# Half of the context's weight remainders formed on VectorE instead of GpSimd, in a two-layer RWKV-7 and neighbourhood-attention block

## The chip, the cores and the metric

One core of one Trainium2 chip runs the whole program in one launch. The metric is the device time of that launch in microseconds, as the median of the runs shown. Engines are named as in the profile: PE is TensorE's matrix multiply, PEld its weight load, DVE is VectorE, ACT is ScalarE, POOL is GpSimd, SP is SyncE, which issues most of the DMAs.

## The reference, cut to what matters

Two layers work on 512 latent tokens (`x`) and, in the first layer only, on 256 context tokens (`ctx`), both 1024 wide. Layer 0 projects both streams with the same weights, scans them in both directions (RWKV-7, 12 heads), projects back and runs a SwiGLU feed-forward net; layer 1 is neighbourhood attention of the latents, with the context's keys and values in the same softmax, and a feed-forward net again.

```python
def swiglu(h, w1, w3, w2):
    return (jax.nn.silu(h @ w1) * (h @ w3)) @ w2
...
    p_lat = h @ w_in
    p_ctx = hc @ w_in
...
        if want_ctx:
            xc = layer_norm(ALPHA * xc + gc_m * yc, ln_g[i, 0], ln_b[i, 0])
            hc = xc * (1.0 + scc_f) + shc_f
            xc = layer_norm(ALPHA * xc + gc_f * swiglu(hc, ffn_w1[i], ffn_w3[i], ffn_w2[i]), ln_g[i, 1], ln_b[i, 1])
```

## The kernel before

**Products in three parts.** Every large product is made with operands split in two: a rounded part `hi` (type fp32r) and the remainder `lo = raw - hi`. `mm3` (L118) multiplies `hi*hi` (L123), `hi` of the weights with `lo` of the activations (L124) and `lo` of the weights with `hi` of the activations (L125). So each weight slice, 128 x 512 in most cases (four blocks of 128 rows by 128 columns), takes four steps: a DMA from SP's queue into `wraw`, a copy on ACT into `whi`, a subtraction into `wlo`, and twelve matmuls.

**Two places do this.** In layer 0's projections, `project` (L246) asks `weight` (L113) for the two slices of one column of `w_in`, and `split` (L104) copies on ACT (L109) and subtracts on GpSimd (L110): 23 columns for the context and the same 23 for the latents, 92 slices. `wraw` has three buffers there, `whi` and `wlo` two each. Everywhere else a `Flow` (L844), one for the context and one for the latents, asks its own `weight` (L878) and `fetch` (L883) for slices; it copies on ACT (L887) and subtracts on `self.lo` (L888), which is GpSimd for the context (`stream` is 1) and VectorE for the latents:

```python
        self.lo = kern.nc.gpsimd if stream else kern.nc.vector
...
        self.lo.tensor_tensor(out=lo, in0=raw, in1=hi, op=ALU.subtract)
```

The context's `Flow` has 176 slices with GpSimd: 16 for the output projection (`mixer_out`, L988), 88 for the feed-forward net's `w1` and `w3`, 72 for its `w2` (`ffn`, L1015), whose 22 blocks are taken by 5, 5, 5, 5 and 2. A column of five blocks is a slice of four and one of a single block (128 x 128), one of two blocks is a slice of 128 x 256. `wraw`, `whi` and `wlo` have three buffers each. When the context's keys and values for layer 1 are made, L610 sets its `self.lo` to VectorE.

**What sets the order.** Each piece of work is given a level by `self.level` (L84); the framework (`schedule_with_timeline_sim=True`) simulates the engines and writes a fixed order of instructions for each of them, a lower level first. An engine then runs its own list strictly in order. The stages of layer 0 are written out in `STAGES` (L26) and woven by `emit` (L513): projections of the context, with the RWKV jobs of the context between them, then projections of the latents, with the context's scan. The latents' scan (`chain`, L1273, level 0, and `prep`, L1071, level 2) then runs in six jobs, and the context's `Flow` (level 8, L595) lies beside it as work of low level. Evacuations of its PSUM bank, with two halves under the one tag `s`, are at level 1 (`gated` L904, `sl` L1028 and L1029). The latents' `Flow` follows at level 9.

Of the kernel before, what the change touches and what calls it, by code (L numbers as in the profile page):

```python
# [12 lines left out]
ALU = mybir.AluOpType  # L13
# [3 lines left out]
P = 128  # L17
# [1 line left out]
NX_, NT_, NS_, NAR_, NA1_, NR_, NY_ = 2, 5, 4, 1, 4, 3, 4  # L19
ND_, NK_, NBK_, NGO_, NAW_ = 6, 3, 2, 3, 4  # L20
ADA0 = 12
POOL_LO = 1

SETS = 9 * "0123"

# [48 lines left out]
class Kernel:  # L74
    def __init__(self, ctx, tc, a, out):
        self.ctx, self.tc, self.nc, self.a, self.out = ctx, tc, tc.nc, a, out
        self.now = 0
        self.tail = None
        self.ps = {}
        self.const = ctx.enter_context(tc.tile_pool(name="const", bufs=1))  # L80
        self.wp = ctx.enter_context(tc.tile_pool(name="wp", bufs=2))
# [19 lines left out]
            "p (%s) -> p %s" % (" ".join(names), " ".join(names)), **dict(zip(names, shape))  # L101
        )

    def split(self, raw, shape, tag="w", bufs=2, pool=None):  # L104

        pool = pool or self.split_pool
        hi = pool.tile(shape, F32R, name=tag + "hi", tag=tag + "hi", bufs=bufs)
        lo = pool.tile(shape, F32R, name=tag + "lo", tag=tag + "lo", bufs=bufs)
        self.nc.scalar.copy(out=hi, in_=raw)  # L109
        (self.nc.gpsimd if POOL_LO else self.nc.vector).tensor_tensor(out=lo, in0=raw, in1=hi, op=ALU.subtract)  # L110
        return hi, lo

    def weight(self, src, shape):  # L113
        raw = self.wp.tile(shape, F32, name="wraw", tag="wraw", bufs=3)
        self.nc.sync.dma_start(out=raw, in_=src)
        return self.split(raw, shape, bufs=2)

    def mm3(self, ps, l, r, first, last, after=None):  # L118
        (lh, ll), (rh, rl) = l, r
# [126 lines left out]
    def project(self, h, src, piece, done):  # L246

        off, n, st = piece
        with self.level(self.now - 1):
            w = [self.weight(src[:, 4 * i:4 * i + 4, :], [P, 4, P]) for i in range(2)]  # L250
        t = self.bank("g", (n,))
        for k in range(KD):
            wk = tuple(x[:, k % 4, :] for x in w[k // 4])
            self.mm3(t, wk, h[1 - st](k), k == 0, k == KD - 1)
            yield n / T
        with self.level(self.now - 1):
            done(t)
# [206 lines left out]
    def gemm(self, h, p, piece):  # L464
# [6 lines left out]
        def project(ft, name):  # L471
            t = self.go(name, n)
            yield from self.project(h, a.w_in[ft], piece, self.shift_mix(ft, t))
            nc.sync.dma_start(out=self.rkv_d[ft][st], in_=t)
            return t
        k = yield from project(6 + p, "k")
        with self.level(self.now - 1):
            sq = self.go("sq", n)
            nc.scalar.activation(out=sq, in_=k, func=AF.Square, scale=col)
        yield from project(12 + p, "v")  # L480
        with self.level(self.now - 1):
            pn = self.bank("g", (nt, 2))
            for t in range(nt):
# [6 lines left out]
                scalar2=0.0, op0=ALU.mult, op1=ALU.add,  # L490
            )
        yield from project(p, "r")
        with self.level(self.now - 1):
            pe = self.bank("g", (n,))
# [345 lines left out]
class Flow:  # L840
# [3 lines left out]
    def __init__(self, kern, pool, prefix, off, n, stream, banks, bg, slots, wide=None):  # L844
        self.K, self.nc, self.pool, self.prefix = kern, kern.nc, pool, prefix
        self.ahead, self.ev = (CAHEAD, CEV) if stream else (LAHEAD, LEV_)
        self.off, self.n, self.stream, self.banks, self.bg = off, n, stream, banks, bg
        self.slots, self.turn, self.halves = slots, 0, []
        self.lo = kern.nc.gpsimd if stream else kern.nc.vector
        wide = self.wide = wide or pool  # L850
        self.xz = wide.tile([P, KD, n], F32, name=prefix + "xz")
        self.h = tuple(wide.tile([P, KD, n], F32R, name=prefix + s) for s in ("hhi", "hlo"))
# [24 lines left out]

    def weight(self, src, shape):  # L878
        tile = lambda s, t: self.wide.tile(shape, t, name="w" + s, tag=self.prefix + "w" + s, bufs=self.slots["w" + s])
        with self.K.level(self.ahead):  # L880
            return self.fetch(tile, src, shape)

    def fetch(self, tile, src, shape):  # L883
        raw = tile("raw", F32) if self.stream else self.K.wp.tile(shape, F32, name="wraw", tag="wraw", bufs=3)
        hi, lo = tile("hi", F32R), tile("lo", F32R)
        self.nc.sync.dma_start(out=raw, in_=src)
        self.nc.scalar.copy(out=hi, in_=raw)  # L887
        self.lo.tensor_tensor(out=lo, in0=raw, in1=hi, op=ALU.subtract)  # L888
        return hi, lo

    def column(self, ps, src, nk, act, order=None, after=None):
# [607 lines left out]
```

## Time and profile before

| | |
|---|---|
| runs shown | 2381.03, 2384.98, 2388.77 us; median 2384.98 |
| the profiled execution | 2381.51 us; span 2379.5 us |
| busy share of the span | PE 91%, PEld 73%, DVE 52%, ACT 42%, POOL 28% |
| granted clock of TensorE, mean | 0.937 |
| instructions | 44426 |

The profile's span runs from the first to the last instruction, so 2.0 us of the profiled execution lie outside it. Busy shares are over the whole span; the stages differ, and the windows below give them apart. A row of waits has the engine, line and tile that waited, what ended the wait, the total in us, how often, and the longest.

### The profile page before, as it was taken

Reading aid. Unit: us, or ns where it says so; the run is one execution under the profiler, and the core shown is the slowest. Engines: PE = TensorE matmul, PEld = TensorE weight load, DVE = VectorE, ACT = ScalarE, POOL = GpSimd, SP = SyncE. Lnnn points to the kernel's source line nnn. Section 1 sums busy time; section 2 is a strip of 40 time slices with the busy share of each in tenths; the row PEclk is TensorE's granted clock in tenths of the full one; section 3 lists DMA queues with packets and bytes.
Section 4 is the critical chain, followed back from the end, with each engine's and each line's share of the span. In section 5 each row is a group of like instructions: output and inputs, shape, how many; then the busy total and the mean of one; then the engine's idle time right before and its main releaser. Section 6 shows DMA issues by size and latency. Waiting matters only on the chain.

```text
span 2379.5 us, 44426 instructions
## 1 busy us (share of the span) xinstructions
PE 2163.1 (91%) x16944; PEld 1735.9 (73%) x16944; DVE 1226.7 (52%) x2529; ACT 994.5 (42%) x2075; POOL 660.5 (28%) x643
## 2 busy tenths in 40 slices
PE   6787988889879898979999999998999998999995
PEld 4676666556657777757788887787878876888874
DVE  2666555636746764244534453347556665333343
ACT  3545344444534544334443342224455644322332
POOL 2442213121322433456642310005224442000021
PEclk9889999879879899999999999999999998999997
DMA  7766476666753544576544335332432112333331
GB/s 262 224 187 188 121 205 186 175 176 187 228 142 89 137 128 112 169 233 214 162 150 118 116 120 167 113 91 88 133 105 63 51 63 66 97 92 100 96 90 63
DMA packets 324677, 327.34 MB, mean 138 GB/s; under 512 B 137328, under 2 KB 214768, under 8 KB 324464
## 3 DMA queue, kind: packets, MB, share of 16 engines
q1 hardware_dynamic: 320720, 317.45, 45.1%
q10 hardware_dynamic: 2592, 3.90, 0.5%
q8 instruction: 133, 2.18, 0.4%
q0 software_dynamic: 1152, 3.15, 0.3%
q14 instruction: 80, 0.66, 0.1%
HBM read 280.02 MB, written 42.80 MB: 136 GB/s over the span
## 4 chain that ended last, share of the span: by engine, by line
PE 62%; DVE 6%; DMA 5%; issue 2%; ACT 2%; SPq 1%; POOL 1%; POOLq 0%; ACTq 0%; DVEq 0%
PE y L123 7%; PE y L125 7%; PE y L124 7%; PE w L123 6%; PE w L124 6%; PE w L125 6%; PE s L123 3%; PE s L125 3%; PE s L124 3%; PE s L743 1%; PE w L1157 1%; DMA wraw<-w 1%; PE v L201 1%; PE v L725 1%; PE y L700 1%
## 5 line engine op out<-in xcount | busy, mean ns | idle before, releaser
L887 ACT CAST whi<-wraw 128x512 fp32r<-128x512 f32 (+2 forms) x560 | 330.2, 594 | 674.1 <-PE y L124 261.0
L888 DVE TENSOR_TENSOR wlo<-wraw,whi 128x512 fp32r<-128x512 f32 (+2 forms) x384 | 293.1, 767 | 339.6 <-ACT whi L887 316.1
L888 POOL TENSOR_TENSOR wlo<-wraw,whi 128x512 fp32r<-128x512 f32 (+2 forms) x176 | 202.3, 1155 | 299.4 <-ACT whi L887 270.7
L123 PE MATMUL w<-lhhi,whi 128*128 128x512 f32 x472 | 189.3, 403 | 11.3 <-ACT lhhi L1012 5.8
L110 POOL TENSOR_TENSOR wlo<-wraw,whi 128x512 fp32r<-128x512 f32 x92 | 121.4, 1323 | 280.1 <-ACT whi L109 233.3
L123 PE MATMUL y<-lhhi,whi 128*128 128x512 f32 x488 | 192.3, 394 | 0.5 <-ACT lhhi L752 0.5
L124 PE MATMUL y<-lhlo,whi 128*128 128x512 f32 x488 | 190.7, 391 | 0.0
L125 PE MATMUL y<-lhhi,wlo 128*128 128x512 f32 x488 | 190.6, 391 | 0.0
L124 PE MATMUL w<-lhlo,whi 128*128 128x512 f32 x472 | 186.4, 395 | 1.3 <-DVE lhlo L937 1.1
L125 PE MATMUL w<-lhhi,wlo 128*128 128x512 f32 x472 | 185.6, 393 | 0.1
L913 POOL TENSOR_TENSOR lxz<-lxz,s 128x512 f32<-128x512 f32 x28 | 43.3, 1578 | 508.9 <-ACT s L919 508.9
L123 PE MATMUL s<-chhi,whi 128*128 128x256 f32 x480 | 145.5, 303 | 19.6 <-DVE kclo L616 7.8
L123 PE MATMUL g<-hhi,whi 128*128 128x256 f32 (+1 forms) x368 | 139.1, 378 | 17.4 <-DVE nr L486 4.5
L125 PE MATMUL s<-chhi,wlo 128*128 128x256 f32 x480 | 143.2, 298 | 1.1 <-POOL wlo L888 1.1
L124 PE MATMUL s<-chlo,whi 128*128 128x256 f32 x480 | 143.3, 299 | 0.4 <-DVE chlo L937 0.4
L125 PE MATMUL g<-hhi,wlo 128*128 128x256 f32 (+1 forms) x368 | 135.6, 369 | 2.2 <-POOL wlo L110 2.1
L124 PE MATMUL g<-hlo,whi 128*128 128x256 f32 (+1 forms) x368 | 132.6, 360 | 0.0
L123 PEld LDWEIGHTS s<-chhi,whi 128*128 128x128 f32 x480 | 97.2, 203 | 29.9 <-ACT whi L887 8.8
L123 PEld LDWEIGHTS w<-lhhi,whi 128*128 128x128 f32 x472 | 89.2, 190 | 36.0 <-ACT lhhi L984 7.4
L123 PEld LDWEIGHTS y<-lhhi,whi 128*128 128x128 f32 x488 | 92.1, 189 | 22.1 <-issue 3.0
L124 PEld LDWEIGHTS w<-lhlo,whi 128*128 128x128 f32 x472 | 89.3, 189 | 23.6 <-DVE lhlo L937 4.2
L125 PEld LDWEIGHTS y<-lhhi,wlo 128*128 128x128 f32 x488 | 91.9, 188 | 19.8 <-DVE n L937 0.8
(376 smaller groups left out, 5048.3 us busy)
## 6 DMA issues: line engine op xcount, KB each, us to landing
wraw<-w SPq DMA_DIRECT2D x368, 256.0 KB, 2.6
aw<-ada_w SPq DMA_DIRECT2D x128, 256.0 KB, 4.7
wraw<-w_in SPq DMA_DIRECT2D x92, 256.0 KB, 3.3
bk<-bk SPq DMA_DIRECT2D x72, 256.0 KB, 4.3
wraw<-ada_w SPq DMA_DIRECT2D x64, 256.0 KB, 3.4
wraw<-w_out SPq DMA_DIRECT2D x48, 256.0 KB, 3.0
wraw<-wk SPq DMA_DIRECT2D x32, 256.0 KB, 2.9
wraw<-wv SPq DMA_DIRECT2D x32, 256.0 KB, 3.1
```

The source lines that it names most:

```text
L110: (self.nc.gpsimd if POOL_LO else self.nc.vector).tensor_tensor(out=lo, in0=raw, in1=hi, op=ALU.subtract)
L123: mm(ps, lhsT=lh, rhs=rh, start=first, stop=False)
L124: mm(ps, lhsT=lh, rhs=rl, start=False, stop=False)
L125: self.last = mm(ps, lhsT=ll, rhs=rh, start=False, stop=last)
L201: mm = nc.tensor.matmul(ps[32 * q:32 * q + 32, part], lhsT=self.cs[:, k + q, :], rhs=w[q // step][:, q % step, :], start=k == 0, stop=k > ...
L700: return lambda: mm(banks[j][:, 256 * c:256 * c + 256], lhsT=q[i == 2][hd, cb * P:cb * P + P], rhs=r[i == 1][hd, cs], start=i == 0, stop=i ...
L725: turn = lambda j, i: lambda: nc.tensor.transpose(out=pt[j][:, i, :], in_=s[j][:, i * P:i * P + P], identity=self.ident)
L743: return lambda: mm(po[64 * j:64 * j + 64, :], lhsT=src[:, hc], rhs=sT[j][:, i, :], start=i == 0, stop=i == 3)
L887: self.nc.scalar.copy(out=hi, in_=raw)
L888: self.lo.tensor_tensor(out=lo, in0=raw, in1=hi, op=ALU.subtract)
L913: tt = lambda o, x, y, op, e=V: e.tensor_tensor(out=o, in0=x, in1=y, op=op)
L1157: nc.tensor.matmul(ps[w][hd[h ^ w], c, :], lhsT=bk[hd[h], w, c, :], rhs=LH[0][hd[h], c, :], start=True, stop=True,)
```

## The change

It moves some of the subtractions from GpSimd to VectorE. In `project`, the second of a column's two slices is subtracted on VectorE when the columns are the context's (`st` is 1); the first stays on GpSimd, and so do both of the latents'. In a `Flow`, slices are counted from one, and the odd ones are subtracted on VectorE, the even ones on `self.lo`. For the latents both are VectorE. The constant `POOL_LO`, which was 1, goes. Sizes, buffers, levels, copies and DMAs stay as written.

```diff
-    def split(self, raw, shape, tag="w", bufs=2, pool=None):
+    def split(self, raw, shape, tag="w", bufs=2, pool=None, lo_engine=None):
...
-        (self.nc.gpsimd if POOL_LO else self.nc.vector).tensor_tensor(out=lo, in0=raw, in1=hi, op=ALU.subtract)
+        (lo_engine or self.nc.gpsimd).tensor_tensor(out=lo, in0=raw, in1=hi, op=ALU.subtract)
...
-            w = [self.weight(src[:, 4 * i:4 * i + 4, :], [P, 4, P]) for i in range(2)]
+            w = [self.weight(src[:, 4 * i:4 * i + 4, :], [P, 4, P], self.nc.vector if st and i else None) for i in range(2)]
...
-        self.slots, self.turn, self.halves = slots, 0, []
+        self.slots, self.turn, self.halves, self.tiles = slots, 0, [], 0
...
+        self.tiles += 1
         with self.K.level(self.ahead):
             return self.fetch(tile, src, shape)
...
-        self.lo.tensor_tensor(out=lo, in0=raw, in1=hi, op=ALU.subtract)
+        (self.nc.vector if self.tiles % 2 else self.lo).tensor_tensor(out=lo, in0=raw, in1=hi, op=ALU.subtract)
```

## Rows read from the trace of the kernel before

**Rows 1.** The page: busy time of each engine, and the last chain by engine.

```profile
PE 2163.1 (91%) x16944; PEld 1735.9 (73%) x16944; DVE 1226.7 (52%) x2529; ACT 994.5 (42%) x2075; POOL 660.5 (28%) x643
...
PE 62%; DVE 6%; DMA 5%; issue 2%; ACT 2%; SPq 1%; POOL 1%; POOLq 0%; ACTq 0%; DVEq 0%
```

**Rows 2.** Windows: PE, PEld, DVE, ACT, POOL busy; PE's clock, DMA share, GB/s.

```profile
0.00:230.00 230.00, 175.64 (x1544) 140.91 (x1544) 128.95 (x310) 106.68 (x249) 77.41 (x72) 0.89 0.72 217
...
660.00:1080.00 420.00, 362.24 (x4826) 298.83 (x4826) 216.96 (x588) 181.91 (x414) 164.68 (x179) 0.88 0.52 147
1080.00:1400.00 320.00, 316.91 (x1810) 269.39 (x1809) 152.99 (x222) 133.62 (x248) 142.21 (x124) 1.00 0.47 144
...
660.00:720.00 60.00, 43.88 (x706) 34.25 (x707) 32.29 (x83) 20.52 (x48) 16.97 (x23) 0.74 0.46 124
720.00:780.00 60.00, 54.91 (x870) 45.55 (x871) 39.61 (x120) 28.56 (x72) 18.00 (x20) 0.91 0.36 96
```

**Rows 3.** Groups of POOL by form: busy us, mean ns, idle time before and its releasers.

```profile
L888 POOL TENSOR_TENSOR wlo<-wraw,whi 128x512 fp32r<-128x512 f32 x136 | 181.0, 1335 | 217.9 <-ACT whi L887 193.8 <-PE s L125 8.9 <-DMA gt<-gate 6.3
L110 POOL TENSOR_TENSOR wlo<-wraw,whi 128x512 fp32r<-128x512 f32 x92 | 121.4, 1323 | 280.1 <-ACT whi L109 233.3 <-PE g L125 10.1 <-PE g L484 8.3
...
L888 POOL TENSOR_TENSOR wlo<-wraw,whi 128x256 fp32r<-128x256 f32 x8 | 6.2, 779 | 22.2 <-ACT whi L887 22.2
```

**Rows 4.** Line L888 on VectorE (later stages): shortest, median, longest in ns; forms.

```profile
L888 DVE TENSOR_TENSOR wlo<-wraw,whi x384: 416/692/1784, 1060.8 to 2341.5; 128x512 fp32r<-128x512 f32 x180, 128x384 fp32r<-128x384 f32 x8, 128x256 fp32r<-128x256 f32 x4
```

**Rows 5.** Timeline 65.5 to 71 us: start, us, instruction, idle before it.

```profile
65.74 2.67 POOL L110 TENSOR_TENSOR wlo<-wraw,whi 128x512 fp32r<-128x512 f32 x2 [1.30 <-PE g L124]
65.78 1.51 DVE L409 TENSOR_TENSOR kds<-kds,k 128x256 f32<-128x256 f32 x1 [1.54 <-DMA k<-rkv]
67.21 1.48 DVE L409 TENSOR_TENSOR bk<-bk,k 128x256 f32<-128x256 f32 x1
68.61 0.41 DVE L409 TENSOR_TENSOR bk<-kds,Pi 128x256 f32<-128x256 f32 x1
...
70.56 0.35 PE L123 MATMUL g<-hhi,whi 128*128 128x256 f32 x1 [4.50 <-DVE k L497]
```

**Rows 6.** Groups from 660 to 1080 us: three DVE by form, POOL all forms.

```profile
L1345 DVE TENSOR_TENSOR z<-z,gt 128x256 f32<-128x256 f32 x12 | 8.4, 696 | 10.4 <-DMA gt<-gate 8.8 <-POOL z L1381 1.5
L1108 DVE TENSOR_TENSOR lh<-kk,Pt 128x256 f32<-128x256 f32 x12 | 6.4, 536 | 12.9 <-DMA Pt<-pt 7.7 <-PE y L1293 5.2
L1345 DVE TENSOR_TENSOR v<-v,w 128x256 f32<-128x256 f32 x12 | 5.0, 419 | 16.1 <-PE w L1370 11.0 <-DMA v<-rkv 3.1 <-PE s L125 2.0
...
L888 POOL TENSOR_TENSOR wlo<-wraw,whi 128x512 fp32r<-128x512 f32 x94 | 108.5, 1160 | 160.5 <-ACT whi L887 133.5 <-PE s L125 8.9 <-DMA gt<-gate 6.3
```

**Rows 7.** Waits of PE from 0 to 230 us: total, times, longest.

```profile
PE w L1157 <- DVE lh L1109: 8.9, 2, 5.6
...
PE g L123 <- DVE k L497: 4.5, 1, 4.5
...
PE g L125 <- POOL wlo L110: 2.1, 4, 1.0
```

**Rows 8.** Waits of PE from 660 to 1080 us.

```profile
PE s L123 <- ACT whi L887: 8.0, 3, 6.7
PE s L123 <- DVE sl L1029: 6.5, 4, 3.0
...
PE s L123 <- DVE cxz L904: 4.8, 5, 1.8
...
PE s L125 <- POOL wlo L888: 1.4, 3, 0.9
```

**Rows 9.** Waits of POOL from 660 to 1080 us.

```profile
POOL wlo L888 <- ACT whi L887: 133.5, 52, 9.8
```

**Rows 10.** Waits of POOL from 0 to 230 us.

```profile
POOL wlo L110 <- ACT whi L109: 96.2, 31, 37.8
```

More of the change, by code (lines that the diff above doesn't have):

```diff
@@ L21 @@
 ADA0 = 12
-POOL_LO = 1
 SETS = 9 * "0123"
@@ L109, in split, with weight @@
         self.nc.scalar.copy(out=hi, in_=raw)
-        (self.nc.gpsimd if POOL_LO else self.nc.vector).tensor_tensor(out=lo, in0=raw, in1=hi, op=ALU.subtract)
+        (lo_engine or self.nc.gpsimd).tensor_tensor(out=lo, in0=raw, in1=hi, op=ALU.subtract)
         return hi, lo
-    def weight(self, src, shape):
+    def weight(self, src, shape, lo_engine=None):
         raw = self.wp.tile(shape, F32, name="wraw", tag="wraw", bufs=3)
         self.nc.sync.dma_start(out=raw, in_=src)
-        return self.split(raw, shape, bufs=2)
+        return self.split(raw, shape, bufs=2, lo_engine=lo_engine)
     def mm3(self, ps, l, r, first, last, after=None):
```

## The prediction, made before the changed kernel was seen

> **What bounds the kernel now.** I read the page first: TensorE is busy 91% of the span and holds 62% of the last chain, GpSimd 1% [rows 1]. So a subtraction counts only where TensorE stands still or runs at a low clock. The windows say where that is [rows 2]: from 0 to 230 us (the context's projections) TensorE is idle for 230 - 175.6 = 54.4 us at a granted clock of 0.89, from 660 to 1080 us (the latents' scan, with the context's flow as filling) for 420 - 362.2 = 57.8 us at 0.88. From 1080 to 1400 us, where the rest of the context's flow runs, it is idle for 3.1 us at 1.00: nothing done to GpSimd or VectorE there can be worth more than that. Then I read the waits of TensorE in the two idle stretches. GpSimd's remainders end only 2.1 and 1.4 us of them directly [rows 7, 8]. VectorE ends far more: its four largest rows make 8.9 + 4.5 + 6.5 + 4.8 = 24.7 us [rows 7, 8].
>
> The timeline ties the two together [rows 5]. While GpSimd makes two remainders in 2.67 us, two VectorE operations on 256 columns take 1.51 and 1.48 us, though their neighbour of the same form takes 0.41 us right after: each ended as GpSimd did. Their 2.2 us of excess stand in the queue ahead of the `k` for which TensorE then waits 4.5 us. Later groups show the same in their means [rows 6]: with both inputs in SBUF, `z<-z,gt` and `lh<-kk,Pt` average 696 and 536 ns, while `v<-v,w`, of the same form with one input in PSUM, averages 419. So a remainder on GpSimd holds up VectorE as well.
>
> **The change part by part.** *Moved.* In the projections 23 of 92 subtractions move, all before about 230 us. In the context's flow the odd slices move: 8 of the output projection, 44 of `w1` and `w3`, 32 of `w2`'s full slices (its single blocks are the even ones and stay) and 4 of 256 columns. GpSimd loses 84 x 1.335 + 23 x 1.323 + 4 x 0.779 = 146 us [rows 3]. VectorE gains 107 x 0.692 + 4 x 0.416 = 76 us, by the durations of the same line for the latents [rows 4]. No DMA, copy or buffer is added. The latents' flow is untouched, as both branches are VectorE there.
>
> *The shorter step.* A moved remainder is ready 1.335 - 0.692 = 0.64 us earlier. The direct waits are 3.5 us in all and about half of the slices move: I take -1.7 us, with bounds 0 and -3.5. `wraw` comes free earlier too, but 6.7 of the 8.0 us that TensorE waits for `whi` are one wait [rows 8], at the flow's first slice, for which no buffer was awaited: I take nothing. What covers that is the three buffers; were they the limit, 1.3 us would be to be had.
>
> *VectorE's delays.* From 660 to 1080 us remainders hold GpSimd for 108.5 of 420 us, 1.16 us each [rows 6]. An SBUF operation that starts at any moment meets one with 26% and then waits half of it: 0.15 us on average. With half of them moved, that is 0.075 us, and 47 remainders of 0.692 us on VectorE itself, 8% of the window, add 0.08 x 0.35 = 0.03 us: a third less. Of the 24.7 us in the four rows a third is 8.2 us; not all of it comes from being held up, so I take -4, with bounds 0 and -8. The added 76 us of work find room: VectorE is idle for 230 - 129 = 101 and 420 - 217 = 203 us in the two stretches [rows 2]. If that cover is gone, the operations behind pay; this is the slower rival.
>
> *The clock.* The two stretches lose 230 x 0.11 + 420 x 0.12 = 76 us of full speed [rows 2], if TensorE was the limit in them. Some 6 of 112 us of idle time are taken away above, 5%; 5% of 76 is 4. Bounds 0 and -4, I take -2. What is late next is mostly ACT's and the DMAs' work, which the change leaves alone.
>
> *Sum.* -1.7 - 4 - 2 = -7.7 us against the profiled execution's 2381.5, so 2373.8. That execution lies 3.5 us under the median of 2384.98, so on the level of the median the sum gives 2377. The bounds alone give 2369 to 2385.
>
> **The rivals.** *Hidden (about 2385).* TensorE takes other work while VectorE is late, so a third off VectorE's delays shows nowhere, and the two stretches end as they do now. For it: GpSimd's direct waits are small and 3.1 us are idle after 1080 us. Against it: the 4.5 us in which TensorE found no other work [rows 5]. A page says as much in advance: the Trainium skill, Perfetto Trace Analysis, section Optimizing Scalar/DVE Operations, warns that moving work between GpSimd and VectorE might not help, as they share an SBUF read port. By it alone the sum would be 2385; the means and the timeline agree that the two hold each other up [rows 5, 6], but also that a remainder holds for 0.69 us instead of 1.33 us when VectorE makes it.
>
> *VectorE's queue stands behind `whi` (slower, about 2397).* The order of an engine's list is fixed by a planner, and an instruction that waits holds all behind it. GpSimd waited for ACT's `whi` for 133.5 us before 52 slices and for 96.2 us before 31 [rows 9, 10], 2.6 and 3.1 us each, with little behind it. If half of these waits stand in VectorE's list, that is 26 x 2.57 + 15 x 3.1 = 113 us, with the scan's updates, the evacuations of `s` and `k` behind them. TensorE stood idle 112 us for 304 us of VectorE's idle time in the two stretches, 0.37 of it; so 113 us cost 42 us at most. The planner places a remainder where it believes `whi` to be done, so I take under half, +20, and with the gain of 8 the time is 2397. It decides from 113 x 0.19 = 21 us of such waits in front of urgent work, as 21 x 0.37 eats the gain. For it speaks how late ACT was; against it, that VectorE has a third to two fifths of its time free.
>
> *A new order that falls well (about 2365).* The planner redraws every list from the first moved subtraction on, far beyond the slices. How much hangs on the order is seen where the flow begins: from 660 to 720 us TensorE is busy 43.9 us at 0.74, in the next 60 us 54.9 us at 0.91 [rows 2]. If the first came out like the second, 11 us of idle time would go. Such a gain on top of half of the sum is 2365 to 2370. A redraw may as well lose so much; that is within the slower rival's range.
>
> That the change does not do what it says can be left aside: the engine is named in the call; only that the moved slices of the flow are the first of a pair, not the second, is to be noted.
>
> **How the numbers follow.** A measurement of this kernel can tell about 0.3%, 7 us, from no change; so faster means under 2378. The forecast of 2377 lies near that edge. Chances: forecast 0.31 (2370 to 2378), the lucky order 0.14 (under 2370), hidden 0.30 (2378 to 2392), the stalled queue 0.25 (over 2392). Faster is 0.31 + 0.14 = 0.45, the same 0.30, slower 0.25. The range reaches from 2358, half of the lucky order's chance below its price, to 2402, a little above the price of the slower rival; that leaves out some 0.2. The forecast's own range is 2369 to 2385.
>
> **What would show it.** Right: 69 subtractions at L110's place and 88 at L888's on GpSimd; TensorE's waits for `k`, `lh`, `sl` and `cxz` shrink from 24.7 us; `z<-z,gt` and `lh<-kk,Pt` fall toward 419 ns; TensorE idles some 6 us less in the two stretches, at a clock no lower. Wrong, hidden: those means fall and the two stretches end at the same times. Wrong, slower: VectorE's remainders between 660 and 1080 us wait for `whi` for tens of us, and TensorE's waits for VectorE grow. Wrong at the root: a difference of over 5 us arises after 1400 us, where no slice was moved, or where only the order differs.

## The result, and the profile after

| | before | after |
|---|---|---|
| runs shown | 4, median 2383.99 us (2381.03 to 2388.77) | 4, median 2417.05 us (2400.84 to 2420.47) |
| ratio, 95% interval | | 1.0124 [1.009, 1.0158] |
| the profiled execution | 2381.51 us, span 2379.5 | 2413.99 us, span 2412.2 |
| mean granted clock | 0.937 | 0.929 |

The kernel is slower: by 33 us of the medians, and by 1.2% in the ratio, which is some 30 us. The forecast was 2377 us with a range to 2402; the time lies above it. Lines have shifted: `mm3` is now L122 to L124, `split` copies at L108 and subtracts at L109, a `Flow` at L888 and L890, and `inverse` and `chain` stand two lines further down.

The page first: busy times, and the last chain by engine [rows 1] (a name with a q is the engine's sequencer).

```profile
PE 2167.7 (90%) x16944; PEld 1743.3 (72%) x16944; DVE 1256.8 (52%) x2640; ACT 992.3 (41%) x2075; POOL 519.6 (22%) x532
...
PE 54%; DMA 5%; DVE 4%; ACT 1%; SPq 1%; issue 1%; POOL 1%; POOLq 0%; DVEq 0%; ACTq 0%
```

GpSimd lost 141 us of work and 111 instructions, VectorE gained 30 us net and the same 111. TensorE's busy time is the same within 5 us, but the span is 33 us longer: for some 28 us more TensorE stands still. The groups of GpSimd's remainders [rows 3]:

```profile
L109 POOL TENSOR_TENSOR wlo<-wraw,whi 128x512 fp32r<-128x512 f32 x69 | 89.5, 1298 | 301.0 <-ACT whi L108 263.0 <-PE g L124 16.9 <-DMA kk<-kk 6.5
L890 POOL TENSOR_TENSOR wlo<-wraw,whi 128x512 fp32r<-128x512 f32 x52 | 68.3, 1314 | 199.1 <-ACT whi L888 184.7 <-DMA L<-ar 7.5 <-PE s L124 5.5
```

These are 69 and, with 32 of 128 x 128 and 4 of 128 x 256 (rows not shown), 88. So the change did what it says. Where the time went, the windows show, first of after, then of before for the two stretches that the prediction did not look at (columns as in [rows 2]):

```profile
0.00:230.00 230.00, 181.09 (x1642) 145.94 (x1643) 133.33 (x336) 107.12 (x253) 46.32 (x50) 0.87 0.69 214
230.00:660.00 430.00, 356.09 (x3716) 261.19 (x3715) 232.82 (x604) 176.60 (x424) 83.16 (x78) 0.86 0.61 174
660.00:1080.00 420.00, 361.91 (x4772) 297.56 (x4771) 235.47 (x644) 181.39 (x418) 102.00 (x123) 0.88 0.49 136
1080.00:1400.00 320.00, 309.69 (x1793) 262.50 (x1792) 161.54 (x251) 131.26 (x242) 97.52 (x91) 0.99 0.51 156
```

```profile
230.00:660.00 430.00, 378.63 (x3892) 274.41 (x3891) 251.60 (x636) 188.29 (x450) 92.26 (x84) 0.89 0.64 182
```

From 0 to 230 us and from 660 to 1080 us, where most of the slices moved, TensorE is as busy as before or busier. (Behind 660 us equal times no longer hold equal work, as the kernel is late by then.) The hole is between: 230 to 660 us, 22.5 us less work at a clock of 0.86 instead of 0.89. That stretch holds the latents' projections, the context's RWKV jobs and the first of the latents'. Not one subtraction was moved there. That the loss is complete at its end shows in the starts of three groups of matmuls (first and last start in us), before and then after:

```profile
L123 PE MATMUL y<-lhhi,whi x488: 387/389/796, 1105.5 to 2284.0; 128*128 128x512 f32 x163
L123 PE MATMUL s<-chhi,whi x480: 274/283/583, 681.8 to 1684.4; 128*128 128x256 f32 x160
L123 PE MATMUL g<-hhi,whi x368: 276/392/797, 39.0 to 658.2; 128*128 128x256 f32 x92, 128*128 128x512 f32 x92
```

```profile
L122 PE MATMUL y<-lhhi,whi x488: 387/389/796, 1124.8 to 2317.7; 128*128 128x512 f32 x163
L122 PE MATMUL s<-chhi,whi x480: 277/283/582, 712.0 to 1713.0; 128*128 128x256 f32 x160
L122 PE MATMUL g<-hhi,whi x368: 276/392/988, 36.9 to 689.8; 128*128 128x256 f32 x92, 128*128 128x512 f32 x92
```

The last projection matmul (`g`) starts 31.6 us later, although the first starts 2 us earlier; the first product of the context's flow (`s`) starts 30.2 us late, and the last of the latents' flow (`y`) 33.7 us late. Where in that stretch the time goes shows when it is cut at 570 us, where 912 of the 1104 projection matmuls (46 columns of 24) are done in both kernels. Before, then after:

```profile
230.00:570.00 340.00, 298.10 (x3394) 213.16 (x3394) 188.84 (x497) 143.32 (x346) 63.97 (x60) 0.88 0.61 173
570.00:658.20 88.20, 79.25 (x497) 60.49 (x495) 62.44 (x138) 44.11 (x102) 28.29 (x24) 0.92 0.76 221
```

```profile
230.00:570.00 340.00, 286.24 (x3290) 207.93 (x3288) 180.12 (x486) 138.59 (x335) 61.92 (x60) 0.87 0.58 166
570.00:689.80 119.80, 93.36 (x510) 69.02 (x511) 69.60 (x161) 50.92 (x122) 27.57 (x24) 0.83 0.66 196
```

Up to 570 us TensorE has run 1544 + 3394 = 4938 matmuls before and 1642 + 3290 = 4932 after, and was busy for 473.7 and 467.3 us: the kernels are level within some 6 us. The rest of the projections then takes 88.2 us before and 119.8 us after, for about as many matmuls. So most of the 31.6 us are lost here. 17.5 us of them are idle time (26.4 against 9.0); in the others TensorE is busy for longer, at a clock of 0.83 instead of 0.92. The waits of TensorE from 230 to 690 us, after:

```profile
PE g L200 <- DMA wraw<-ada_w: 18.7, 12, 6.1
PE w L1239 <- DMA T<-td: 13.2, 6, 6.9
PE w L1159 <- issue: 7.6, 2, 6.1
...
PE w L1159 <- DVE X L1194: 5.5, 1, 5.5
...
PE c L1287 <- DVE ST L1326: 3.8, 1, 3.8
PE c L1304 <- ACT g L1289: 3.2, 2, 2.6
```

The largest row is no difference: before, it is 20.1 us. Before, in the same stretch, the same two products of the RWKV jobs:

```profile
PE w L1157 <- DVE lh L1109: 1.4, 2, 0.9
...
PE w L1237 <- DMA T<-td: 0.4, 1, 0.4
```

L1239 (before: L1237) is the first product of `inverse`. Its operand `T` is made on VectorE, written to HBM and read back in another layout, so it comes by a DMA. The wait for that DMA grew from 0.4 to 13.2 us. One place shows such a wait (trace of after, 356 to 368 us: start, duration, instruction, idle time before it):

```profile
356.65 0.39 PE L124 MATMUL g<-hhi,wlo 128*128 128x512 f32 x1
...
362.23 0.36 PE L1239 MATMUL w<-T,A 64*64 64x64 f32 x1 [2.31 <-DMA T<-td]
...
363.08 1.97 PE L1239 MATMUL w<-T,A 64*64 64x64 f32 x32 [0.16 <-DMA T<-td]
...
365.05 1.91 PE L1239 MATMUL w<-T,A 64*64 64x64 f32 x30
...
367.94 0.80 PE L122 MATMUL g<-hhi,whi 128*128 128x512 f32 x1
```

This is the third inverse, the last of the context's. Between the projection matmul at 356.65 and the next at 367.94 us TensorE does small products and waits for `T`; the weights of the next slice had been ready since about 359 us, so its twelve matmuls could have run. In the kernel before, this first product stands behind 763 of the 1104 projection matmuls; after, behind 708. The planner drew TensorE's list anew and put it 55 matmuls earlier.

So the theory is: not the engine of the subtractions costs the time but the redrawn order, and in it mainly the early place of the context's inverses in TensorE's list. The rivals: VectorE's longer queue (the prediction's slower rival), and some other part of the redrawn lists.

For the second half of the theory the trace speaks only weakly. All six waits for `T` end before 570 us, where the kernel is still nearly level. The third inverse has 2.5 us of them; the longest stands at the fourth inverse, the first of the latents', which is behind 840 projection matmuls in both kernels and is reached 8 us earlier after than before:

```profile
480.61 0.47 PE L1239 MATMUL w<-T,A 64*64 64x64 f32 x2 [6.95 <-DMA T<-td]
```

```profile
488.53 0.47 PE L1237 MATMUL w<-T,A 64*64 64x64 f32 x2 [0.41 <-DMA T<-td]
```

Behind 570 us, where the time is lost, the two longest waits stand at L1159, a product of the latents' next RWKV jobs; before, the longest at this product (L1157) in that stretch is 0.9 us:

```profile
581.03 2.88 PE L1159 MATMUL w<-lh,bk 64*64 64x128 f32 x32 [5.47 <-DVE X L1194]
615.50 2.89 PE L1159 MATMUL w<-lh,bk 64*64 64x128 f32 x32 [6.06 <-issue]
```

So the experiments have to show whether the inverses' place leads to this, or another part of the lists.

### The profile page after: what moved, and what is told of

Same layout as the page of the kernel before. It is cut to its first block, busy times and chain, and to the rows that moved or that the text cites. A ratio compares the mean times of both kernels' runs of the same rounds, so it can differ in the third digit from the quotient of the medians.

```text
span 2412.2 us, 44492 instructions
## 1 busy us (share of the span) xinstructions
PE 2167.7 (90%) x16944; PEld 1743.3 (72%) x16944; DVE 1256.8 (52%) x2640; ACT 992.3 (41%) x2075; POOL 519.6 (22%) x532
## 4 chain that ended last, share of the span: by engine, by line
PE 54%; DMA 5%; DVE 4%; ACT 1%; SPq 1%; issue 1%; POOL 1%; POOLq 0%; DVEq 0%; ACTq 0%
PE y L122 7%; PE y L124 7%; PE y L123 7%; PE w L122 6%; PE w L123 6%; PE w L124 6%; PE s L122 3%; PE s L124 2%; PE s L123 2%; PE v L200 1%; PE s L743 1%; PE v L725 1%; PE y L700 1%; DMA aw<-ada_w 1%; DVE n L939 1%
## 5 line engine op out<-in xcount | busy, mean ns | idle before, releaser
L888 ACT CAST whi<-wraw 128x512 fp32r<-128x512 f32 (+2 forms) x560 | 329.5, 592 | 663.6 <-PE y L123 279.6
L890 DVE TENSOR_TENSOR wlo<-wraw,whi 128x512 fp32r<-128x512 f32 (+2 forms) x472 | 351.0, 747 | 403.4 <-ACT whi L888 395.7
L122 PE MATMUL w<-lhhi,whi 128*128 128x512 f32 x472 | 190.1, 404 | 9.8 <-ACT lhhi L1014 4.9
L122 PE MATMUL y<-lhhi,whi 128*128 128x512 f32 x488 | 192.1, 394 | 0.5 <-ACT lhhi L752 0.5
L124 PE MATMUL y<-lhhi,wlo 128*128 128x512 f32 x488 | 190.3, 391 | 0.0
L124 PE MATMUL w<-lhhi,wlo 128*128 128x512 f32 x472 | 185.3, 393 | 0.2 <-DVE wlo L890 0.2
L122 PE MATMUL s<-chhi,whi 128*128 128x256 f32 x480 | 144.5, 301 | 20.8 <-DVE kclo L616 7.9
L890 POOL TENSOR_TENSOR wlo<-wraw,whi 128x512 fp32r<-128x512 f32 (+2 forms) x88 | 88.9, 1012 | 324.3 <-ACT whi L888 274.0
L109 POOL TENSOR_TENSOR wlo<-wraw,whi 128x512 fp32r<-128x512 f32 x69 | 89.5, 1298 | 301.0 <-ACT whi L108 263.0
L122 PE MATMUL g<-hhi,whi 128*128 128x256 f32 (+1 forms) x368 | 141.0, 384 | 11.1 <-DVE nr L486 6.0
L124 PE MATMUL s<-chhi,wlo 128*128 128x256 f32 x480 | 142.2, 296 | 0.0
L124 PE MATMUL g<-hhi,wlo 128*128 128x256 f32 (+1 forms) x368 | 135.7, 369 | 1.8 <-POOL wlo L109 1.8
L122 PEld LDWEIGHTS s<-chhi,whi 128*128 128x128 f32 x480 | 96.2, 200 | 27.5 <-DVE kclo L616 8.3
L122 PEld LDWEIGHTS w<-lhhi,whi 128*128 128x128 f32 x472 | 89.3, 190 | 35.3 <-ACT lhhi L986 6.5
L122 PEld LDWEIGHTS y<-lhhi,whi 128*128 128x128 f32 x488 | 92.0, 188 | 22.6 <-ACT whi L888 2.8
L108 ACT CAST whi<-wraw 128x512 fp32r<-128x512 f32 x92 | 56.8, 618 | 122.5 <-DMA wraw<-w_in 62.4
L1159 PE MATMUL w<-lh,bk 64*64 64x128 f32 x1152 | 88.4, 313 | 20.7 <-issue 7.9
```

Source lines behind the costliest of these rows:

```text
L109: (lo_engine or self.nc.gpsimd).tensor_tensor(out=lo, in0=raw, in1=hi, op=ALU.subtract)
L122: mm(ps, lhsT=lh, rhs=rh, start=first, stop=False)
L124: self.last = mm(ps, lhsT=ll, rhs=rh, start=False, stop=last)
L890: (self.nc.vector if self.tiles % 2 else self.lo).tensor_tensor(out=lo, in0=raw, in1=hi, op=ALU.subtract)
L1159: nc.tensor.matmul(ps[w][hd[h ^ w], c, :], lhsT=bk[hd[h], w, c, :], rhs=LH[0][hd[h], c, :], start=True, stop=True,)
```

## The experiments

In each, the subtractions that may move are the 23 in `project` and the 88 in `Flow`, 111 in all. Where a list is held, the kernel is built twice, and edges without a semaphore make the planner keep the other build's order. Two numbers often given together in the expectations are the places of the third inverse's first product (L1239) and of its later one (L1259); where a text calls the second one "the fourth", that later product is meant.

**Engine or order?** The first kernel has the new engines in the old order of every engine; the second has the old engine in the changed kernel's order.

```diff
+    plan = build(arrays, 0, 0, None)[1]
+    nc, _ = build(arrays, 1, 1, plan)
...
+                if engine in last:
+                    tc.add_manual_dep(i, last[engine], ... NoSync ..., reason="plan")
+                last[engine] = name
```

> All 111 subtractions are made on VectorE as in the change, but every engine's list is held to the order of the kernel before: TensorE, ScalarE and SyncE have the very same lists, and a moved subtraction stands in VectorE's list where it stood in the common order. Theory O (the redrawn order costs the time): the loss is gone, 2372 to 2391 us, and the projections of the latents end at about 660 us as before. Theory Q (VectorE's list stands behind whi and behind 76 us of added work): the loss stays, 2400 to 2425 us, with VectorE's remainders waiting for whi for tens of us.

> The other corner: every engine's list is held to the order of the changed kernel, but all subtractions of the context are made on GpSimd as before. Theory O: the loss is here although no work has moved, 2405 to 2430 us, and the projections of the latents end at about 690 us. Theory Q: without the work on VectorE the loss goes, 2375 to 2392 us.

Measured: 2376.23 us, ratio 0.9987 [0.9957, 1.0017], for the new engines in the old order; 2415.11 us, 1.016 [1.0106, 1.0215], for the old engine in the new order. The second has the waits of the changed kernel again, in the same stretch:

```profile
PE w L1239 <- DMA T<-td: 12.6, 6, 6.5
PE w L1159 <- issue: 7.0, 1, 7.0
...
PE w L1159 <- DVE X L1194: 5.6, 1, 5.6
```

The order alone makes the whole loss; the engines alone make none. The place is the same too: from 570 us to the last projection matmul it is 120.4 us with the old engine in the new order, and 86.7 us with the new engines in the old one (88.2 before, 119.8 after). The prediction's slower rival falls with it. Its sign was that VectorE waits for `whi` by tens of us from 660 to 1080 us. The row is there in the changed kernel, and there again in the first experiment, which is not slower:

```profile
DVE wlo L890 <- ACT whi L888: 32.5, 18, 4.4
```

```profile
DVE wlo L890 <- ACT whi L888: 36.1, 23, 3.7
```

**Which of the two places?** Only the projections' 23, then only the flow's 88, with all lists redrawn freely.

```diff
-            w = [self.weight(src[:, 4 * i:4 * i + 4, :], [P, 4, P], None) for i in range(2)]
+            w = [self.weight(src[:, 4 * i:4 * i + 4, :], [P, 4, P], self.nc.vector if st and i else None) for i in range(2)]
```

```diff
-        self.lo.tensor_tensor(out=lo, in0=raw, in1=hi, op=ALU.subtract)
+        (self.nc.vector if self.tiles % 2 else self.lo).tensor_tensor(out=lo, in0=raw, in1=hi, op=ALU.subtract)
```

> Only the projections' second slices move (23 of 111), lists drawn anew; the context's flow keeps GpSimd. Theory O: the lists differ from the first moved slice on, so the loss before 690 us can come back nearly whole, 2400 to 2425 us. Theory Q: the loss goes with the number of moved slices and lies before 230 us, where they are: 23/111 of 33 us is 7 us, so 2387 to 2395 us.

> Only the odd slices of the context's flow move (88 of 111), lists drawn anew; TensorE's list is the one of before until the flow begins at about 680 us. Theory O: no loss before 680 us, and after it a redraw of a stretch that TensorE fills anyway, 2372 to 2395 us. Theory Q: 88/111 of 33 us is 26 us, all between 680 and 1400 us, so 2405 to 2415 us.

Measured: 2407.15 us, 1.0116 [1.0065, 1.0167], for the projections; 2379.57 us, 0.9985 [0.9953, 1.0017], for the flow. The first shows 13.9 us of waits for `T` at L1239 from 230 to 690 us, and takes 117.0 us from 570 us to its last projection matmul; the second keeps TensorE's old list up to the flow. So the 23 subtractions made before 230 us cost some 28 us, most of them lost behind 570 us, and the 88 of the flow cost nothing that shows.

**How little is enough?** One subtraction of the 111 is moved: that of the 17th context column, then that of the 11th.

```diff
+    def one(self, st, i):
+        self.seen = getattr(self, "seen", -1) + (1 if st and i else 0)
+        return self.nc.vector if st and i and self.seen in ONLY else None
```

> One subtraction of 111 moves to VectorE, the second slice of the 17th of the context's 23 projections; lists drawn anew. 0.7 us of work has moved. In TensorE's new list the third inverse's first product stands behind 712 of the projections' matmuls (before: 763, in the changed kernel: 708), as in the changed kernel. Theory T: the time is that of the changed kernel, 2400 to 2420 us. Theory L, or work that had moved: no loss, 2375 to 2390 us.

> One subtraction moves as well, the second slice of the 11th projection; lists drawn anew. TensorE's list differs from the one before in as many places, but the third inverse's first product stands behind 758 of the projections' matmuls, about as before. Theory T with the place of the inverses as the cause: no loss, 2370 to 2392 us. If any redraw costs: 2400 us or more.

Measured: 2412.53 us, 1.0142 [1.0099, 1.0185], and 2378.76 us, 0.9987 [0.9968, 1.0005]. One subtraction of 0.7 us makes as great a loss as all 111, another none. What differs is the list: the third inverse stands behind 712 projection matmuls in the first, behind 758 in the second. (The first inverse, early after the change at 362 instead of 408, is at 408 in both of these.) The slow one waits differently from the changed kernel: 7.8 us for `TT` and 4.5 us for `T`, both of which come from HBM, and from 570 to 690 us one wait of 9.4 us for a slice of `ada_w`.

**Is it TensorE's list alone?** All 111 are moved and only TensorE's list is held to the old one.

```diff
+                if not engine.endswith("PE"):
+                    continue
```

> All 111 subtractions on VectorE; TensorE's list alone is held to the order of the kernel before, the lists of the other engines are drawn anew. Theory T (the loss is in TensorE's list: products stand ahead of others that were ready): 2370 to 2392 us. Theory L (it is in the lists that feed TensorE: SyncE's loads, ScalarE's copies): the loss stays in good part, 2395 to 2420 us.

Measured: 2395.55 us, 1.0055 [1.0034, 1.0076]. About half of the loss is gone, and with it the inverse's waits (`T` 0.5 us). What is left arises early in the execution that was profiled, which at 2406.87 us was the slowest of the six: from 0 to 230 us the clock is 0.82 instead of 0.89 [rows 2], and these waits stand there (the first was 4.4 us before):

```profile
PE g L565 <- DVE pooled L561: 10.6, 2, 6.0
PE g L124 <- DVE wlo L109: 5.5, 3, 2.7
```

The third inverse starts 19 us late here (398.3 us, 379.0 before) and the last projection matmul 22 us (680.4, 658.2): with TensorE's old list almost nothing is lost between them, so the late loss goes with TensorE's list. But here this list was not as good beside lists that were not drawn with it: holding one and redrawing the rest had a price of its own.

**Is it the inverse's place?** Next, only that place is held: all 111 are moved, every list is redrawn, and edges keep each first product of the context's inverses behind the projection matmul that it followed in the kernel before.

```diff
+                if i is not None and name in PROJECTIONS:
+                    behind = name
+                if name in INVERSE:
+                    tc.add_manual_dep(i, behind, ... NoSync ..., reason="plan")
```

> The changed kernel with all 111 subtractions on VectorE, lists drawn anew, but the first products of the context's inverses may not be issued ahead of the projection matmul that they followed in the list of before (edges on TensorE alone). Theory T with the place of the inverses as the cause: most of the loss goes, 2372 to 2395 us, and the waits of the inverse's product for the landing of T, some 13 us in the changed kernel, fall to under 4. If those waits are only a sign of something else: 2400 to 2420 us.

Measured: 2373.04 us, 0.9952 [0.9932, 0.9972], faster than both kernels. The wait for `T` is down to 2.0 us, and from 570 us to the last projection matmul it is 88.7 us, as before the change. Then the reverse, on the kernel before: no subtraction is moved, and the projection matmul that follows an inverse's first product in the changed kernel's list may not come ahead of it.

```diff
+                if name in PROJECTIONS and ahead:
+                    tc.add_manual_dep(i, ahead, ... NoSync ..., reason="plan")
+                    ahead = None
```

> All subtractions are GpSimd's, as before; the lists are redrawn with one thing held: the context's inverses' first products stand ahead of the projection matmul that they precede in the changed kernel's list (the third behind 710 of 1104 projection matmuls, the fourth behind 737; 763 and 768 in the kernel before). If the early place of the inverses makes the loss, it is lost here without any subtraction being moved: 1.008 to 1.016, 2400 to 2420 us, with TensorE's waits for T at the inverse's first product of some 10 us between 230 and 700 us. If the subtractions' engine is needed for the loss, or the place is only a sign of something else in the lists, 0.998 to 1.004.

Measured: 2405.36 us, 1.0101 [1.0079, 1.0124]. With the early place 24 us are lost without any subtraction moved. One part of the expectation failed: the wait for `T` is one of 4.4 us, before 230 us, and L1239 has no such wait at all from 230 to 690 us. The last projection matmul starts at 670.5 us, 12.3 us late, so this kernel shows the change's delay of 31.6 us there only in part; the rest of its loss comes later. TensorE is less busy behind the inverses instead, from 440 to 540 us, and later at 690 to 1080 us (341 us against 344). The first of these windows, in this kernel:

```profile
440.00:540.00 100.00, 78.09 (x814) 54.13 (x815) 47.70 (x133) 36.57 (x91) 15.27 (x16) 0.74 0.60 172
```

and in the kernel before:

```profile
440.00:540.00 100.00, 82.90 (x897) 55.94 (x897) 50.44 (x150) 40.01 (x98) 16.60 (x16) 0.78 0.59 168
```

In the third of this group the places of all the context's inverses in the new engines' kernel are shifted one column of 24 matmuls further back.

```diff
-                    tc.add_manual_dep(i, behind, ... NoSync ..., reason="plan")
+                    tc.add_manual_dep(i, line[at + 8], ... NoSync ..., reason="plan")
```

> e8 with each of the context's inverses' first products held 24 projection matmuls (one column) further back than in the kernel before: the third behind 786, the fourth behind 816. If TensorE still waits for T in e8 (2.0 us for T, 3.1 for TT), a later place takes that away, 0.992 to 0.995 (2363 to 2371 us). If the kernel before's place is about right and what hangs on the inverse is urgent (the state of the context's RWKV), the later place costs: 0.998 to 1.006. A monotone gain with lateness would say that only the waits count; a rise says that there is a best place.

Measured: 2392.86 us, 1.0048 [1.0029, 1.0067]. Later is worse as well, although the wait for `T` is gone. That the state which hangs on the inverse is late was the expectation's reason; no row shows it as the cost. By the place of the third inverse's first product (the kernel with TensorE's list alone held, 763 and 1.0055, is the exception told above; the 786 has all the context's inverses shifted):

| projection matmuls ahead of it | ratios to before |
|---|---|
| 708 to 712 | 1.0124 (after), 1.016, 1.0116, 1.0142, 1.0101 |
| 758 to 763 | 1 (before), 0.9987, 0.9985, 0.9987, 0.9952 and, from the runs below, 0.9997, 0.9959 |
| 786 | 1.0048 |

In every kernel but one the place goes with the time. That makes it a good mark of a bad draw; it does not show that the time is lost there.

**What are the engines worth, then?** The last two ask whether the faster kernel owes its 0.5% to its order or to VectorE. One has its lists, engine by engine, with all subtractions on GpSimd; the other is that kernel once more.

```diff
+    plan = build(arrays, 1, 1, plan)[1]
+    nc, _ = build(arrays, 0, 0, plan, True)
```

> Every engine's list is the one of e8, but all subtractions are GpSimd's again. If the order alone makes e8 faster than the kernel before, this kernel keeps nearly all of e8's 0.9952: 0.994 to 0.998, some 2371 to 2378 us. If the engine is what made e8 faster (the prediction's VectorE term, -4 us, now that the order is no longer in the way), it falls back to 0.999 to 1.002, and z<-z,gt and lh<-kk,Pt are slower here than in e8.

> The kernel of e8 once more, beside other runs of the kernel before: e8 (0.9952) and e9, the same lists with GpSimd (0.9997), were measured at different times, and the profiled execution of e8 was its slowest. If the moved subtractions are worth something once the order is right, this gives 0.993 to 0.9975 again, 2365 to 2376 us. If e8's gain was a matter of the occasion, 0.998 to 1.001, 2377 to 2384 us, and the engine is worth nothing in either order.

Measured: 2381.3 us, 0.9997 [0.9977, 1.0017], with GpSimd, and 2366.33 us, 0.9959 [0.994, 0.9979], for the repetition. The gain is confirmed, and in these lists it belongs to the engines. In the repetition the window behind the projections has TensorE at a higher clock than in the kernel with GpSimd, its row second, and than before (0.89):

```profile
690.00:1080.00 390.00, 341.88 (x4570) 291.28 (x4569) 219.31 (x594) 174.60 (x397) 104.20 (x124) 0.92 0.52 151
```

```profile
690.00:1080.00 390.00, 343.15 (x4560) 292.93 (x4561) 199.78 (x541) 173.19 (x395) 162.82 (x170) 0.91 0.52 150
```

The two executions shown have spans of 2368.3 and 2375.0 us; 0.01 of clock over 390 us is 4 us, within what single executions of one kernel differ by, so the trace does not place the gain.

## Why the prediction was wrong

**The step that failed** is "a new order", which stood among the rivals, as a gain of 11 us of idle time from 660 to 720 us, with the remark that a redraw may as well lose so much and that the slower rival's range covers it. The premise was right: the planner redraws every list from the first moved subtraction on. Its size and its place were not, and the loss was named in that remark alone. It cost 31.6 us by the end of the projections, not 11, and most of it arose between 570 and 690 us, a stretch for which the prediction read no window, since no slice is moved there. The sum of the forecast has no term for the order at all: it was put at nothing. A chance of its own, 0.14, went to the gain only; a redraw that loses was left to the slower rival, whose 0.25 was worked out from VectorE's queue. Of the conditions that the text gave for "wrong at the root", the second came true: a difference of over 5 us arose where only the order differs.

**The slower rival** had the right sign and the wrong mechanism. It took 113 us of waits for `whi` in VectorE's list and under half of what these might cost; those found are 22.8 us in 0 to 230 us, the row below, and 32.5 us in 660 to 1080 us. By the prediction's own factor of 0.37 these would cost 20 us. They cost nothing that can be seen: the first experiment, 0.9987, has 28.4 and 36.1 us of them, and the faster kernel's repetition 26.4 and 44.5 us. That the planner puts a remainder where little that is urgent stands behind it would explain this, but no run shows it.

```profile
DVE wlo L109 <- ACT whi L108: 22.8, 10, 6.2
```

**The sum of -7.7 us** was meant for an unchanged order, and for that case the runs bear it out as far as they can. Four pairs differ in the engine alone at equal lists: 0.9987 (-3 us), after against the old engine in its order 1.0124 / 1.016 = 0.9965 (-8 us), 0.9952 / 0.9997 = 0.9955 (-11 us) and 0.9959 / 0.9997 = 0.9962 (-9 us). All have the sign of the forecast, and -7.7 us is 0.9968. The first interval includes no change, and so does the second with some 0.006; for the last two, each ratio's interval of 0.002 makes some 0.003 for the quotient, which excludes it, but these two are one kernel measured twice, divided by the same run. The lists of the last three were drawn for the new engines, which may favour them. How the sum divides among its three terms is open: no run took them apart. In the first experiment, with the old lists, the four waits of 24.7 us (for `k`, `lh`, `sl` and `cxz`) are 4.1 + 8.8 + 4.7 + 5.3 = 22.9 us, a fall of 1.8 where the sum took 4. TensorE is idle there for 47.2 + 52.9 = 100.1 us in the two stretches, 12 us less and not 6, but at a clock of 0.87 in both, lower than before, where the sum took 2 us from a better clock.

The Trainium skill, Perfetto Trace Analysis, section Optimizing Scalar/DVE Operations, warns that a move between GpSimd and VectorE might not help, as they share an SBUF read port. If such a move did not help at all, these pairs would be at 1. The last two are not, by little more than their uncertainty, so here the move helped by some 0.4%, in lists drawn for it.

**The indicators.** The counts 69 and 88 are right, and GpSimd's 146 us came out as 141. From 660 to 1080 us the mean of `z<-z,gt` fell from 696 to 508 ns, as forecast, that of `lh<-kk,Pt` only from 536 to 530. Over the whole span `z<-z,gt` fell from 605 to 480 ns, yet most of this is the order: with the old engine in the new order it is 489 ns, and with the new engines in the old order 568. What the engine does at equal lists shows better in VectorE's busy time. In the first experiment it is 1264.5 us against 1226.7, 38 us more, though the remainders on it take 77 us more (370 against 293), so the rest of its busy time falls by some 39 us. After against the old engine in its order it is 40 us for 73, and in the faster kernel's lists 42 us for 81. So in all three pairs VectorE's other work gets shorter when remainders leave GpSimd, as the prediction said; TensorE's time gains little by it.

**What stays open.** That the order makes the loss is shown, both ways. That the inverses' place steers it is shown by holding it (a loss of 1.2% turned into a gain of 0.5%) and by bringing it about (1.0%), but each edge also redraws the rest, and no run moves this place alone. How the place leads to the loss is not shown: after the change most of the time is lost behind 570 us, with the longest waits at L1159, and not at the inverses' waits for `T`, behind which the kernel is nearly level; with one late slice moved the longest wait there is for `ada_w`; with the early place forced, the projections end only 12.3 us late. Which part of the redrawn lists costs how much was not taken apart. A run that holds the products L1159 of the latents' jobs behind the projection matmuls that they followed before, and leaves the inverses free, would be the next test.

## What to carry to other kernels

Where a planner writes the engines' lists from simulated times, a change of one small instruction is two changes: the instruction, and a new draw of the order from there on. Take them apart before judging either: build once with the old order held, once with the new order and the old instruction. When the draw turns out badly, look for a group of products whose place in TensorE's list goes with the time over several draws, and hold it; here this made the change worth 0.4 to 0.5% instead of costing 1.2%. And before a wait is named as the cause, count the work done on both sides of it: here the waits that had grown most stood ahead of a point at which little had been lost yet.

## What the runs showed that was not expected

The order was worth more here than the edit: one subtraction of 0.7 us moved among 44,426 instructions makes 1.0142, and another one, six columns earlier, 0.9987. Most of the loss does not arise where TensorE's list first differs after the change, behind some 55 us, but 500 us later. And both directions cost: the draws with the third inverse some 50 projection matmuls earlier lose 1.0 to 1.6%, the one with the context's inverses a column later 0.5%.
